# A gated decoder block on one core: the linear recurrence by products of decays, and steps moved between operands and their users

## The chip, the cores and the metric

One Trainium2 chip, one of its cores. The metric is the device time of one execution in microseconds. The core's engines are named as in its profile: PE (TensorE, matmuls; PEld its weight loads), DVE (VectorE), ACT (ScalarE), POOL (GpSimd) and SP (SyncE, which here only issues the loads of weights).

## What is computed

One layer of a decoder block for 256 positions of width 2048, in float32. The part that the change rewrites is the second branch, a gated linear recurrence with 8 heads and 128 keys and values each. Cut to what matters:

```python
a = rmsnorm(h, norm_mix_pre)
q_a, k_a, v_a, q_r, f_r, i_r, g_r, gate_a, gate_r = split(a @ w_in)
# attention: three head groups with windows and dilations, rotary q and k
q = silu(q_r); f = lb + (1 - lb) * sigmoid(f_r)
# S_t = diag(f_t) S_{t-1} + (1 - f_t) v_t^T ;  o_t = S_t^T q_t
r = rmsnorm_per_head(o) * gain * silu(g_r)
y = sigmoid(gate_a) * (attn @ w_pa) + sigmoid(gate_r) * (r @ w_pr)
h = h + rmsnorm(y @ w_o)
h = h + rmsnorm(swiglu(rmsnorm(h)))
```

Without the state, o_t is a sum over all s up to t of (q_t · D(t, s) · k_s) v_s, where D(t, s) is, for each of the 128 keys, the product of the decays f between s and t. Both kernels compute the 256 x 256 matrix of these scores block by block and multiply it with v.

## The kernel before

**Weights.** Nearly all the time goes into products of activations with weights that come from memory once. Each float32 factor is split into a high part (rounded to PE's fp32r format) and the rest, and three of the four partial products are computed. SP loads weights `N_RAW` = 3 units ahead. `split` makes the high part on ACT (L297, `w<-raw`) and the low part on DVE (L298, `w<-raw,w`), two steps ahead of their use (`AHEAD`), into three buffers (`N_SPLIT`). So ACT's split of step n+2 can begin when PE has finished step n-1.

**Blocks and steps.** A block is one slice of a weight matrix. Kind "N" has activations as the stationary operand and 512 columns of weights moving. Kind "W" (the forget gate f, the recurrence's q, and q and k of the attention) has 128 x 128 weights as the stationary operand and positions moving, so that the result stands with channels on the partitions. For each weight tile of a "W" block there is a pair of matmuls (L319 to L321): the high part times both halves of x (512 columns), then the low part times the high half of x (256 columns). One step of "W" is 4 x 2 pairs. "Wide" blocks use a seven-product scheme for 2 x 2 tiles.

**The order of the work** is the order in which the main loop (L1390 to L1421) writes it: for each step first the split of step n+2, then the matmuls of step n, then one advance of each queue of smaller work. `evacs` holds the evacuations of finished blocks, `turns` the transposes of y, and two lanes hold the longer jobs: the opening (norm of x, gates' bounds), the two halves of the recurrence (lane 0) and the eight attention heads (both lanes, as they come free). These jobs are generators: a `yield` ends what is written after one step. Every engine runs its own instructions strictly in the order written.

**The recurrence** (L840 to L1017, one call for four heads): `kk` = 1 - f; f is bounded below (L853), its logarithm taken (L855), and summed within blocks of 64 by a scan on DVE (L857) into `b`. For each block size w = 1, 2, ... 32 (`level`, L861) POOL subtracts the value at the block's middle (L865), ACT takes exponentials (L868, L869), DVE multiplies the left half by kk (L871) and POOL the right half by q (L872); 8 matmuls follow, and DVE copies the scores under a mask into `at` (L883). `level64` and `level128` do the same for the larger distances; `same` (L946) gives the diagonal: q times kk on POOL (L949), summed over the keys by a matmul with a column of ones, and copied under the identity as a mask (L955). A new level begins every second advance, so that two or three are under way. Then come the products with v, the norm (L143 to L151), the gate and the transposes into `recT`.

**Other places that the change touches.** `evac_f` (L717, L718) and `evac_qr` (L734, L735) multiply on DVE and take a sigmoid on ACT at once. `evac_g` (L750 to L756) makes the gate g and stores it to memory from ACT's queue (L756); its multiply L755 needs the row `gainr` from memory. `evac_rope` (L776, L783, L784) writes q and k of the attention (`qk`) and, after the last of a pair of heads, starts `attention`, whose first instructions are matmuls on `qk`. `evac_attn_branch` (L1038, L1039) makes y and hands it to the transposes (L482) in the same step.

Of the kernel before, what the change touches and what calls it, by code (L numbers as in the profile page):

```python
# [30 lines left out]
F_MIN = 2.0 ** -63  # L31
# [60 lines left out]
def tile_hybrid_block(ctx: ExitStack, tc: tile.TileContext, t, out):  # L92
# [100 lines left out]
    def fslot(s):  # L193
        return pool["now"].tile([P, 1024], F32, tag="f", bufs=15, name=nm(s))
# [8 lines left out]
    reset = kp.tile([P, 1024], F32, name="reset")  # L203
    nc.gpsimd.memset(reset, 1.0)
    nc.gpsimd.memset(reset.rearrange("p (n w) -> p n w", w=64)[:, :, 0:1], 0.0)
# [94 lines left out]
    def multiply(st):  # L300
# [257 lines left out]
    def flush_lanes():  # L558
        while work or lanes[0] or lanes[1]:
            advance_lanes()  # L560

# [147 lines left out]
    def evac_f(half):  # L709
        def ev(i, src):  # L710
# [6 lines left out]
            nc.vector.tensor_mul(in_time(d), by_side(src), by_side(by_rows(rowb, 2)))  # L717
            nc.scalar.activation(d, d, AF.Sigmoid)  # L718
# [9 lines left out]
    def evac_qr(half, then=None):  # L728
        def ev(i, src):
# [4 lines left out]
            nc.vector.tensor_mul(in_time(d), by_side(src), by_side(by_rows(rowb, 2)))  # L734
            nc.scalar.activation(s, d, AF.Sigmoid)  # L735
# [6 lines left out]
    def evac_g(half):  # L742
        def go(banks):
# [3 lines left out]
            for i in range(2):  # L747
# [8 lines left out]
                nc.scalar.dma_start(there[:, i, :], dst[:, i, :])  # L756
# [35 lines left out]
    def attention(pair, hh):  # L792
        o, head = None, 2 * pair + hh
        while (head // 4, 2) not in vN:
# [45 lines left out]
    def recurrence(half):  # L840
        q, f, g = qT[half], fT[half], gN[half]
# [3 lines left out]
        def spans(x, w):  # L845
            return x.rearrange("p (n w) -> p n w", w=w)

        kk, b, at = fslot("kk"), fslot("b"), fslot("at")
# [4 lines left out]
        nc.vector.tensor_scalar(f, f, F_MIN, None, op0=OP.max)  # L853
        yield
        nc.scalar.activation(f, f, AF.Ln)  # L855
        yield
        nc.vector.tensor_tensor_scan(  # L857
            out=b, data0=reset, data1=f, initial=0.0, op0=OP.mult, op1=OP.add,
        )
        yield  # L860
        def level(lev, w):  # L861
            x = fslot("x")
            xv, bv, kv, qv = (spans(a, 2 * w) for a in (x, b, kk, q))
            n = 1024 // (2 * w)
            nc.gpsimd.tensor_sub(xv, bv, bv[:, :, w - 1 : w].to_broadcast([P, n, 2 * w]))  # L865
            yield
            left, right = slice(0, w), slice(w, 2 * w)
            nc.scalar.activation(xv[:, :, left], xv[:, :, left], AF.Exp, scale=-1.0)  # L868
            nc.scalar.activation(xv[:, :, right], xv[:, :, right], AF.Exp)  # L869
            yield  # L870
            nc.vector.tensor_mul(xv[:, :, left], xv[:, :, left], kv[:, :, left])  # L871
            nc.gpsimd.tensor_mul(xv[:, :, right], xv[:, :, right], qv[:, :, right])  # L872
            yield
            yield
            ps = aux()
            for e in range(8):
                xe = x[:, e * P : (e + 1) * P]
                mm(
                    spans(ps[:, e * 64 : (e + 1) * 64], w), xe,
                    spans(xe, 2 * w)[:, :, right], True, True,  # L880
                )
            yield
            nc.vector.copy_predicated(  # L883
                at.rearrange("p (e n w) -> p e n w", e=8, w=2 * w)[:, :, :, right],
                lmask[:, lev, :].rearrange("p (n w) -> p n w", w=w)[:, None, :, :]
                .to_broadcast([P, 8, 64 // w, w]).bitcast(I32),
                ps.rearrange("p (e n w) -> p e n w", e=8, w=w),
            )

        def level64():  # L890

            x = fslot("x")
            xe, be, ke, qe = (
                a.rearrange("p (e c t) -> p e c t", e=8, c=2) for a in (x, b, kk, q)
            )
            nc.gpsimd.tensor_sub(
                xe[:, :, 0, :], be[:, :, 0, :], be[:, :, 0, 63:64].to_broadcast([P, 8, 64])
            )
            yield
            nc.scalar.activation(xe[:, :, 0, :], xe[:, :, 0, :], AF.Exp, scale=-1.0)  # L900
            nc.scalar.activation(xe[:, :, 1, :], be[:, :, 1, :], AF.Exp)
            yield
            nc.vector.tensor_mul(xe[:, :, 0, :], xe[:, :, 0, :], ke[:, :, 0, :])
            nc.gpsimd.tensor_mul(xe[:, :, 1, :], xe[:, :, 1, :], qe[:, :, 1, :])
            yield
            ps = aux()
            for e in range(8):
                mm(ps[:64, e * 64 : (e + 1) * 64], xe[:, e, 0, :], xe[:, e, 1, :], True, True)
            yield
            nc.scalar.activation(  # L910
                at.rearrange("p (e t) -> p e t", e=8)[:64, :, 64:],
                ps[:64].rearrange("p (e t) -> p e t", e=8), AF.Copy,
            )

        def level128():

            x = fslot("x")
            xc, bc = (a.rearrange("p (h c t) -> p h c t", h=4, c=4) for a in (x, b))
            end = small("end")
            nc.vector.tensor_add(end[:, :4], bc[:, :, 0, 63], bc[:, :, 1, 63])  # L920
            nc.vector.tensor_sub(
                xc[:, :, 0, :], bc[:, :, 0, :], end[:, :4, None].to_broadcast([P, 4, 64])
            )
            nc.gpsimd.tensor_sub(
                xc[:, :, 1, :], bc[:, :, 1, :], bc[:, :, 1, 63:64].to_broadcast([P, 4, 64])
            )
            nc.gpsimd.tensor_add(
                xc[:, :, 3, :], bc[:, :, 3, :], bc[:, :, 2, 63:64].to_broadcast([P, 4, 64])
            )
            yield  # L930
            xh, kh, qh = (a.rearrange("p (h t) -> p h t", h=4) for a in (x, kk, q))
            nc.scalar.activation(xh[:, :, :P], xh[:, :, :P], AF.Exp, scale=-1.0)
            nc.scalar.activation(xc[:, :, 2, :], bc[:, :, 2, :], AF.Exp)
            nc.scalar.activation(xc[:, :, 3, :], xc[:, :, 3, :], AF.Exp)
            yield
            nc.vector.tensor_mul(xh[:, :, :P], xh[:, :, :P], kh[:, :, :P])
            nc.gpsimd.tensor_mul(xh[:, :, P:], xh[:, :, P:], qh[:, :, P:])
            yield
            ps = aux()
            for h in range(4):  # L940
# [544 lines left out]
```

## Time and profile before

| | us |
|---|---|
| three runs | 1752.32, 1753.49, 1754.23 |
| the profiled execution | 1753.41 |
| its span in the profile | 1751.3 |

Rows of the trace name the source line, the engine, the operation and the tiles (`out<-in`). A busy PE includes matmuls whose ends are modelled. "Idle before" is the time an engine stood still before an instruction, with the line whose end released it.

### The profile page before, as it was taken

The numbers are of one execution on the slowest core, as the hardware profiler recorded it, in microseconds if no ns is written. First come the engines' busy times: TensorE is split into PE (matmuls) and PEld (weight loads), VectorE is DVE, ScalarE is ACT, GpSimd is POOL, SyncE is SP. The second block draws the span as 40 slices with busy tenths as digits, with TensorE's granted clock in tenths as the row PEclk, the third lists the DMA queues.
The fourth block names the chain that finished last, engine by engine and source line by source line (L and its number), as shares of the span: only waits on it lengthen the run. The fifth ranks groups of instructions, "written<-read, shape, count | busy, mean of one in ns | idle before, by whom it ended". The sixth has DMA issues, their size and how long they took to land.

```text
span 1751.3 us, 21627 instructions
## 1 busy us (share of the span) xinstructions
PE 1716.4 (98%) x8357; PEld 1438.6 (82%) x8357; DVE 1382.7 (79%) x1457; ACT 925.6 (53%) x1051; POOL 92.5 (5%) x72
## 2 busy tenths in 40 slices
PE   9999999999989899999999999999999999999997
PEld 7788888888878798888887877888888888888886
DVE  6668888885777897776656467888888888898998
ACT  6445555554645444444444456555555555565663
POOL 0000000000241341000000000000000000000000
PEclk9999999999999999999999999999999999999999
DMA  7766666666535445565545745555555555666553
GB/s 262 248 232 210 224 216 232 235 229 228 166 123 168 158 135 192 166 216 174 181 153 166 264 168 193 192 194 203 204 198 206 197 192 192 216 217 215 189 197 120
DMA packets 208998, 344.78 MB, mean 197 GB/s; under 512 B 10960, under 2 KB 77696, under 8 KB 208896
## 3 DMA queue, kind: packets, MB, share of 16 engines
q1 hardware_dynamic: 198848, 319.41, 54.0%
q10 hardware_dynamic: 7456, 14.56, 2.2%
q0 software_dynamic: 2592, 9.44, 1.6%
q8 instruction: 65, 1.06, 0.2%
q14 instruction: 37, 0.30, 0.1%
HBM read 331.83 MB, written 11.53 MB: 196 GB/s over the span
## 4 chain that ended last, share of the span: by engine, by line
PE 90%; DVE 4%; ACT 2%; issue 1%; POOL 1%; DMA 0%; ACTq 0%; SPq 0%; DVEq 0%; POOLq 0%
PE acc L133 57%; PE aux L133 32%; DVE w L298 1%; ACT w L297 1%; PE aux L821 0%; PE aux L494 0%; DVE x L871 0%; POOL x L865 0%; PE acc L1178 0%; DVE fz L1305 0%; DVE b L857 0%; DMA x<-in_x 0%; PE aux L1178 0%; PE aux L482 0%; DVE sum L783 0%
## 5 line engine op out<-in xcount | busy, mean ns | idle before, releaser
L298 DVE TENSOR_TENSOR w<-raw,w 128x1024 fp32r<-128x1024 f32 (+1 forms) x225 | 279.3, 1243 | 194.2 <-ACT w L297 193.7
L133 PE MATMUL acc<-xT,w 128*128 128x512 f32 (+1 forms) x2048 | 376.4, 343 | 2.9 <-DVE w L298 2.4
L297 ACT ACTIVATE w<-raw 128x1024 fp32r<-128x1024 f32 (+1 forms) x225 | 236.1, 1053 | 254.0 <-PE acc L133 228.0
L133 PEld LDWEIGHTS acc<-xT,w 128*128 128x128 f32 x2048 | 316.2, 190 | 48.8 <-DVE w L298 3.0
L333 DVE TENSOR_TENSOR wl<-raw,w 128x2048 fp32r<-128x2048 f32 x125 | 285.7, 2287 | 62.1 <-ACT w L331 61.1
L331 ACT ACTIVATE w<-raw 128x2048 fp32r<-128x2048 f32 x125 | 238.7, 1910 | 129.8 <-PE aux L133 60.0
L349 DVE TENSOR_TENSOR wl<-sum,w 128x2048 fp32r<-128x2048 f32 x63 | 144.4, 2291 | 65.0 <-ACT w L345 64.9
L133 PE MATMUL acc<-w,hT 128*128 128x512 f32 x622 | 182.5, 392 | 1.5 <-DVE w L298 1.2
L133 PE MATMUL acc<-w,xT 128*128 128x512 f32 x536 | 158.2, 398 | 2.3 <-ACT w L297 1.8
L342 ACT ACTIVATE w<-sum 128x1024 fp32r<-128x1024 f32 x63 | 67.0, 1063 | 172.1 <-DVE sum L337 161.8
L133 PEld LDWEIGHTS acc<-w,hT 128*128 128x128 f32 x622 | 115.8, 188 | 26.9 <-DVE w L298 2.5
L133 PE MATMUL aux<-w,hT 128*128 128x512 f32 x430 | 135.7, 389 | 0.0
L133 PEld LDWEIGHTS acc<-w,xT 128*128 128x128 f32 x536 | 101.9, 192 | 24.5 <-ACT w L297 2.0
L133 PE MATMUL aux<-w,xT 128*128 128x512 f32 x386 | 121.1, 390 | 0.0
L351 DVE TENSOR_TENSOR dl<-raw,dh 128x1536 fp32r<-128x1536 f32 x63 | 110.3, 1751 | 0.0
L133 PEld LDWEIGHTS aux<-w,hT 128*128 128x128 f32 x430 | 80.7, 188 | 16.7
L348 ACT ACTIVATE dh<-raw 128x1536 fp32r<-128x1536 f32 x63 | 92.8, 1474 | 0.0
L133 PE MATMUL acc<-w,yT 128*128 128x512 f32 x384 | 88.1, 390 | 0.2 <-DVE w L298 0.2
L133 PEld LDWEIGHTS aux<-w,xT 128*128 128x128 f32 x386 | 72.4, 188 | 15.3 <-ACT w L331 0.3
L133 PEld LDWEIGHTS acc<-w,yT 128*128 128x128 f32 x384 | 71.9, 188 | 15.5 <-DVE w L298 0.6
L133 PE MATMUL aux<-wl,hT 128*128 128x512 f32 x215 | 83.7, 389 | 0.0
L133 PE MATMUL acc<-w,a 128*128 128x512 f32 x268 | 83.7, 389 | 0.0
(281 smaller groups left out, 2778.2 us busy)
## 6 DMA issues: line engine op xcount, KB each, us to landing
raw<-in_w_in SPq DMA_DIRECT2D x271, 512.0 KB, 4.6
raw<-in_w_ffn_gate_up SPq DMA_DIRECT2D x176, 512.0 KB, 4.4
raw<-in_w_ffn_down SPq DMA_DIRECT2D x88, 512.0 KB, 4.8
raw<-in_w_mix_out SPq DMA_DIRECT2D x32, 512.0 KB, 4.9
kept<-e ACTq DMA_DIRECT2D x32, 256.0 KB, 4.5
raw<-in_w_hgrn_branch SPq DMA_DIRECT2D x16, 512.0 KB, 4.4
raw<-in_w_attn_branch SPq DMA_DIRECT2D x16, 512.0 KB, 4.5
v<-kept POOLq DMA_DIRECT2D x8, 512.0 KB, 6.3
```

The lines of the kernel that those rows point to most:

```text
L133: nc.tensor.matmul(ps, lhsT, rhs, start=start, stop=stop, skip_group_check=True)
L297: nc.scalar.activation(wh[:, k], raw[:, k], AF.Copy)
L298: nc.vector.tensor_sub(wl[:, k], raw[:, k], wh[:, k].bitcast(F32))
L331: nc.scalar.activation(hi, raw, AF.Copy)
L333: nc.vector.tensor_sub(lo, raw, hi.bitcast(F32))
L342: nc.scalar.activation(hi[:, :1024], s[:, :1024], AF.Copy)
L348: nc.scalar.activation(dhi, d, AF.Copy)
L349: nc.vector.tensor_sub(lo, s, hi.bitcast(F32))
L351: nc.vector.tensor_sub(dlo, d, dhi.bitcast(F32))
```

## The change

Recurrence: no logarithms, no scan, no sums. `q` and `kk` are kept, in place, multiplied by the decays up to the edge of their block: q first by its own f, then, from block size to block size, the right half's q by the total decay of the left half, and the left half's kk by that of the right half. The totals (`tot`) are products of pairs of totals. So the scores of a level are plain matmuls of `kk` and `q` as they stand at that level. All multiplies are DVE's; POOL keeps one memset per half, and ACT two copies of scores. Levels run one after the other, three advances each. The diagonal comes from full 128-column products of kk and q, of which the identity mask picks the diagonal.

Besides: for every second weight tile of a "W" block the short matmul goes ahead of the long one; a `yield` stands ahead of the sigmoids in `evac_f` and `evac_qr` and at the start of `attention`; the transposes of y are handed over one advance later; g is stored from POOL's queue; the pool of 4 KB tiles has 16 buffers in place of 15 and the constant `reset` is gone; ahead of the second wide block only lane 1 is flushed.

```diff
-                mm(b.banks[s], h, both, first, False)
-                mm(b.banks[s][:, :S], l, xh, False, last)
+                pair = [(b.banks[s], h, both), (b.banks[s][:, :S], l, xh)]
+                for i, (ps, x, y) in enumerate(pair if k % 2 == 0 else pair[::-1]):
+                    mm(ps, x, y, first and i == 0, last and i == 1)
...
# evac_f, evac_qr
             nc.vector.tensor_mul(in_time(d), by_side(src), by_side(by_rows(rowb, 2)))
+            yield
             nc.scalar.activation(d, d, AF.Sigmoid)
...
# evac_g
-                nc.scalar.dma_start(there[:, i, :], dst[:, i, :])
+                nc.gpsimd.dma_start(there[:, i, :], dst[:, i, :])
...
# attention
         o, head = None, 2 * pair + hh
+        yield
...
# recurrence
+        kk, tot, at = fslot("kk"), fslot("tot"), fslot("at")
         nc.gpsimd.memset(at, 0.0)
-        nc.scalar.preload_act_table_set("natural_log_exp_and_others")
         nc.vector.tensor_scalar(kk, f, -1.0, 1.0, op0=OP.mult, op1=OP.add)
         yield
+        yield
+        own = [aux(), aux()]
+        for e in range(8):
+            es = slice(e * P, (e + 1) * P)
+            mm(own[e // 4][:, e % 4 * P : (e % 4 + 1) * P], kk[:, es], q[:, es], True, True)
+        yield
...
+        nc.vector.tensor_mul(q, q, f)
+        yield
+        yield
...
+        a2, t, at0 = [], f, 0
+        for lev in range(8):
+            w = 1 << lev
+            yield from products(lev, w)
+            if w == P:
+                break
...
+            nc.vector.tensor_mul(qv[:, :, w:], qv[:, :, w:], left)
+            yield
+            nc.vector.tensor_mul(kv[:, :, :w], kv[:, :, :w], right)
+            if w < 64:
+                tv = t.rearrange("p (n two) -> p n two", two=2)
+                t, at0 = tot[:, at0 : at0 + n], at0 + n
+                nc.vector.tensor_mul(t, tv[:, :, 0], tv[:, :, 1])
+            yield
+        yield
...
# evac_attn_branch
-                if i == 1:
-                    turns.append(yT[0].turned(y, 2 * j, 2))
                 yield
+            turns.append(yT[0].turned(y, 2 * j, 2))
...
-                  pre=flush_lanes if n == 1 else None)
+                  pre=(lambda: flush(lanes[1])) if n == 1 else None)
```

In `products`, matmuls of `kk` with the right halves of `q` are followed, one advance later, by the masked copy as before.

How the order moves, at three places. First ACT, where the evacuation of q for heads 4 and 5 falls among the levels of the first half. `sum` and `sig` belong to that evacuation, `x` to the levels, `w<-raw` is the split of weights. Before:

```order
L239 ACTIVATE sum_3699<-acc_3557 128x256
L239 ACTIVATE sum_3699<-acc_3558 128x256
L735 ACT_TABLE_LOAD
L735 ACTIVATE sig_3705<-q_3704 128x512
L868 ACT_TABLE_LOAD
L868 ACTIVATE x_3674<-x_3674 128x64x8
L869 ACTIVATE x_3674<-x_3674 128x64x8
L297 ACTIVATE w_3711<-raw_3508 128x1024
L297 ACTIVATE w_3745<-raw_3555 128x1024
```

And now, at the same place:

```order
L235 ACTIVATE sum_3688<-acc_3555 128x256
L235 ACTIVATE sum_3688<-acc_3556 128x256
L293 ACTIVATE w_3698<-raw_3509 128x1024
L730 ACTIVATE sig_3694<-q_3693 128x512
L293 ACTIVATE w_3721<-raw_3553 128x1024
L293 ACTIVATE w_3752<-raw_3553 128x1024
```

The exponentials and the two table loads are gone, and the split of weights stands ahead of the sigmoid instead of behind it.

Second DVE at the same place, where L298 (now L294) is the low part of the split and L883 (now L884) the masked copy. Before:

```order
L883 COPY_PREDICATED at_3402<-lmask,aux_3663 128x256x2
L298 TENSOR_TENSOR w_3711<-raw_3508,w_3711 128x1024
L737 TENSOR_TENSOR q_3704<-q_3704,sig_3705 128x512
L871 TENSOR_TENSOR x_3674<-x_3674,kk_3400 128x64x8
L298 TENSOR_TENSOR w_3745<-raw_3555,w_3745 128x1024
L883 COPY_PREDICATED at_3402<-lmask,aux_3732 128x128x4
```

And now:

```order
L884 COPY_PREDICATED at_3420<-lmask,aux_3656 128x256x2
L919 TENSOR_TENSOR q_3279<-q_3279,tot_3419 128x256x2
L294 TENSOR_TENSOR w_3698<-raw_3509,w_3698 128x1024
L921 TENSOR_TENSOR kk_3418<-kk_3418,tot_3419 128x256x2
L925 TENSOR_TENSOR tot_3419<-tot_3419 128x256
L294 TENSOR_TENSOR w_3721<-raw_3553,w_3721 128x1024
L732 TENSOR_TENSOR q_3693<-q_3693,sig_3694 128x512
L294 TENSOR_TENSOR w_3752<-raw_3553,w_3752 128x1024
L884 COPY_PREDICATED at_3420<-lmask,aux_3743 128x128x4
```

A level has two multiplies and a product of totals on DVE where it had one multiply, and takes three splits where it took two.

Third PE in the second block of the attention's branch, where y of the block before is transposed (L482, now L479). Before:

```order
L133 MATMUL acc_7162<-w_7124,attnT_2967 128x512 x6
L133 MATMUL acc_7163<-w_7124,attnT_2967 128x512 x6
L133 MATMUL acc_7162<-w_7141,attnT_2968 128x512 x6
L133 MATMUL acc_7163<-w_7141,attnT_2968 128x512 x6
L482 MATMUL aux_7205<-ident,y_7184 128x128 x4
L133 MATMUL acc_7162<-w_7157,attnT_2969 128x512 x6
```

And now:

```order
L132 MATMUL acc_7087<-w_7045,attnT_2964 128x512 x6
L132 MATMUL acc_7088<-w_7045,attnT_2964 128x512 x6
L132 MATMUL acc_7087<-w_7066,attnT_2965 128x512 x6
L132 MATMUL acc_7088<-w_7066,attnT_2965 128x512 x6
L132 MATMUL acc_7087<-w_7082,attnT_2966 128x512 x6
L132 MATMUL acc_7088<-w_7082,attnT_2966 128x512 x6
L479 MATMUL aux_7147<-ident,y_7109 128x128 x4
```

The first four transposes stand behind three steps of the block instead of two.

More of the change, by code (lines that the diff above doesn't have):

```diff
@@ L193, in fslot @@
     def fslot(s):
[L194 removed]
+        return pool["now"].tile([P, 1024], F32, tag="f", bufs=16, name=nm(s))
     def ptile(s):
@@ L890, in level64 @@
[L890 to L940, printed above, removed]
-                mm(ps[:, h * P : (h + 1) * P], xh[:, h, :P], xh[:, h, P:], True, True)
-            yield
-            a2.append(ptile("a2"))
-            nc.scalar.activation(a2[0], ps, AF.Copy)
@@ L946, in same @@
-        def same():
-            x = fslot("x")
-            nc.gpsimd.tensor_mul(x, q, kk)
-            yield
-            ps = aux()
-            for e in range(8):
-                mm(ps[:, e : e + 1], x[:, e * P : (e + 1) * P], ones[:, 0:1], True, True)
-            yield
-            nc.vector.copy_predicated(
-                at.rearrange("p (e t) -> p e t", e=8),
-                ident[:, None, :].to_broadcast([P, 8, P]).bitcast(I32),
-                ps[:, :8, None].to_broadcast([P, 8, P]),
-            )
@@ L961, in recurrence @@
-        a2 = []
-        todo = [level(lev, w) for lev, w in enumerate(LEVELS)] + [same(), level64(), level128()]
-        running, turn = [], 0
-        while todo or running:
-            if turn % 2 == 0 and todo:
-                running.append(todo.pop(0))
-            for r in list(running):
-                try:
-                    next(r)
-                except StopIteration:
-                    running.remove(r)
-            turn += 1
-            yield
+        for i, ps in enumerate(own):
+            nc.vector.copy_predicated(
+                at[:, i * 512 : (i + 1) * 512].rearrange("p (e t) -> p e t", e=4),
+                ident[:, None, :].to_broadcast([P, 4, P]).bitcast(I32),
+                ps.rearrange("p (e t) -> p e t", e=4),
+            )
@@ new lines, in recurrence, with products @@
+        yield
+        nc.vector.tensor_mul(q, q, f)
+        yield
+        yield
+        def products(lev, w):
+            ps = aux()
+            if w < 64:
+                for e in range(8):
+                    es = slice(e * P, (e + 1) * P)
+                    mm(
+                        spans(ps[:, e * 64 : (e + 1) * 64], w), kk[:, es],
+                        spans(q[:, es], 2 * w)[:, :, w:], True, True,
+                    )
+                yield
+                nc.vector.copy_predicated(
+                    at.rearrange("p (e n w) -> p e n w", e=8, w=2 * w)[:, :, :, w:],
+                    lmask[:, lev, :].rearrange("p (n w) -> p n w", w=w)[:, None, :, :]
+                    .to_broadcast([P, 8, 64 // w, w]).bitcast(I32),
+                    ps.rearrange("p (e n w) -> p e n w", e=8, w=w),
+                )
+            elif w == 64:
+                for e in range(8):
+                    k0, q0 = e * P, e * P + 64
+                    mm(ps[:64, e * 64 : (e + 1) * 64], kk[:, k0:q0], q[:, q0 : q0 + 64], True, True)
+                yield
+                nc.scalar.activation(
+                    at.rearrange("p (e t) -> p e t", e=8)[:64, :, 64:],
+                    ps[:64].rearrange("p (e t) -> p e t", e=8), AF.Copy,
+                )
+            else:
+                for h in range(4):
+                    k0, q0 = h * S, h * S + P
+                    mm(ps[:, h * P : (h + 1) * P], kk[:, k0:q0], q[:, q0 : q0 + P], True, True)
+                yield
+                a2.append(ptile("a2"))
+                nc.scalar.activation(a2[0], ps, AF.Copy)
```

46 lines of the change are left out of this document (7 added, 39 removed).

## The prediction

> **What bounds the kernel now.** I read first the page's share of each engine, then the list of who waited for whom on TensorE, then a table of seven stretches of the span.
>
> ```profile
> PE 1716.4 (98%) x8357; PEld 1438.6 (82%) x8357; DVE 1382.7 (79%) x1457; ACT 925.6 (53%) x1051; POOL 92.5 (5%) x72
> ```
>
> TensorE (PE) is busy nearly all the time, so a gain can only come out of its idle time, of a slower clock, or of matmuls that follow each other more slowly than they need. VectorE (DVE) is next with 79%, GpSimd (POOL) hardly works at all. The waits of PE (total us, times, longest) say where the idle time is:
>
> ```profile
> PE aux L133 <- DVE qk L784: 7.4, 3, 6.7
> PE acc L133 <- DVE w L298: 4.2, 6, 1.3
> PE aux L133 <- POOL x L949: 3.7, 1, 3.7
> PE aux L482 <- DVE y L1039: 3.6, 4, 0.9
> PE acc L133 <- ACT w L297: 2.3, 2, 1.8
> ```
>
> Every one of these five is a step that the change touches or a weight split that stands behind such a step. The stretches: from:to, their length, busy us of PE, PE's weight loads, DVE, ACT, POOL, then the granted clock, the DMA share and GB/s.
>
> ```profile
> 64.00:440.00 376.00, 376.00 (x1714) 313.01 (x1713) 293.81 (x238) 200.19 (x173) 3.15 (x4) 1.00 0.66 229
> 44.00:64.00 20.00, 15.76 (x53) 11.41 (x52) 13.47 (x27) 9.63 (x11) 0.85 (x1) 0.83 0.57 200
> 472.00:520.00 48.00, 41.12 (x240) 35.59 (x240) 37.27 (x32) 25.47 (x33) 24.57 (x11) 0.93 0.35 111
> 580.00:612.00 32.00, 25.30 (x138) 22.06 (x138) 26.48 (x26) 14.16 (x21) 12.29 (x6) 0.89 0.41 133
> 612.00:700.00 88.00, 88.00 (x577) 79.30 (x576) 73.82 (x97) 40.09 (x75) 27.36 (x18) 1.00 0.49 161
> 700.00:855.00 155.00, 154.32 (x916) 135.88 (x915) 112.97 (x163) 69.80 (x104) 4.33 (x6) 1.00 0.57 187
> 905.00:955.00 50.00, 46.36 (x217) 37.47 (x216) 33.16 (x39) 21.72 (x24) 0.00 (x0) 1.00 0.52 169
> ```
>
> The first row is an undisturbed stretch, and the one at 612 is another: no idle time, full clock. The others lose 4.2, 6.9, 6.7, 0.7 and 3.6 us to waiting; in three the clock is also down, which costs busy time x (1 - clock): 15.76 x 0.17 = 2.7, 41.12 x 0.07 = 2.9, 25.30 x 0.11 = 2.8 us. The stretches at 472 and 580 are the two recurrences, and there POOL is at work; so I compared DVE's instructions between 470 and 720 with those between 735 and 850, where POOL is nearly idle (busy us, mean ns):
>
> ```profile
> L298 DVE TENSOR_TENSOR w<-raw,w 128x1024 fp32r<-128x1024 f32 x67 | 86.7, 1293 | 46.5 <-ACT w L297 46.2
> L776 DVE TENSOR_TENSOR w<-sum,tabs 64x512 f32<-64x512 f32 x28 | 23.5, 838 | 0.8
> L784 DVE TENSOR_TENSOR qk<-sum,w 128x512 f32<-128x512 f32 x13 | 14.6, 1122 | 0.5
> ...
> L871 DVE TENSOR_TENSOR x<-x,kk 128x512 f32<-128x512 f32 x11 | 11.9, 1083 | 0.1
> L883 DVE COPY_PREDICATED at<-lmask,aux 128x512 f32<-128x512 int32 x12 | 11.0, 918 | 0.1
> L737 DVE TENSOR_TENSOR q<-q,sig 128x512 f32<-128x512 f32 x2 | 5.3, 2644 | 0.0
> ...
> L857 DVE TENSOR_TENSOR_SCAN b<-reset,f 128x1024 f32<-128x1024 f32 x1 | 2.3, 2283 | 0.0
> ```
>
> ```profile
> L298 DVE TENSOR_TENSOR w<-raw,w 128x1024 fp32r<-128x1024 f32 x36 | 44.1, 1225 | 33.4 <-ACT w L297 33.4
> L776 DVE TENSOR_TENSOR w<-sum,tabs 64x512 f32<-64x512 f32 x18 | 12.3, 686 | 0.5
> L241 DVE TENSOR_TENSOR sum<-acc,sum 128x256 f32<-128x256 f32 x18 | 6.7, 416 | 0.0
> L784 DVE TENSOR_TENSOR qk<-sum,w 128x512 f32<-128x512 f32 x9 | 6.2, 692 | 0.4
> ```
>
> The same 512-element multiply-add is 692 ns away from POOL and 1122 ns on average beside it, and L737 even 2644 ns. ACT, in turn, waits inside its own queue (stretch 470 to 620) and reloads tables:
>
> ```profile
> ACT x L868 <- POOL x L865: 9.7, 4, 2.6
> ...
> ACT sig L735 <- DVE q L734: 9.0, 2, 4.6
> ```
>
> While ACT stands there, the high half of the next weights (L297) stands behind it, and then DVE's low half (L298), and then PE. That is how the recurrence, off the path itself, reaches PE.
>
> **The change part by part, against the profiled execution's 1753.4 us** (span 1751.3, 2.1 outside it; the median of the runs is 1753.5, the same).
>
> *Recurrence.* Gone: all of POOL's subtractions and products, the scan, Ln and exponentials, 8 of 19 table loads. Added on DVE: a half has 14 multiplies of 512 elements (at L784's 692 ns in the quiet stretch, 9.7 us), one of 1024 (L298's 1225), six shorter ones (together at most 2 us) and two diagonal copies in place of one; gone are the scan (2.3), eight multiplies of 512 (5.5) and two short passes. So DVE's clean work grows by at most 9.7 + 1.2 + 2.0 - 2.3 - 5.5 = 5.1 us a half, and loses the collisions: eleven L871 at 1083 instead of 692 save 4.3 us, thirteen L784 5.6, twenty-eight L776 4.3, two L737 3.9, together some 18 us over both halves. Does DVE keep up? A step of a wide block costs it 1.23 for the split and a quarter of 2 x 0.42 + 4 x 0.69, 2.1 us; a level takes three steps and adds 0.92 + 2 x 0.69 + 0.42 = 2.7: 9.1 us. PE's three steps need three times eight pairs at 0.349 us (below) and the level's 16 passes at 22.9 / 192 = 0.12 us, 10.3 us:
>
> ```profile
> L133 PE MATMUL aux<-x 128*128 128x64 f32 x192 | 22.9, 272 | 0.3 <-DVE x L871 0.2
> ...
> L133 PE MATMUL aux<-ones,x 128*128 128x1 f32 x32 | 5.4, 299 | 3.7 <-POOL x L949 3.7
> ...
> L133 PE MATMUL aux<-x 128*128 128x128 f32 x16 | 2.1, 274 | 0.0
> ```
>
> DVE is then at 88% of PE's time, near, but below. The diagonal's 16 matmuls grow from 1 column to 128, yet 32 passes at 2.1 / 16 = 0.13 us are 4.2 us against 5.4 before: nothing. I take the whole loss of the stretch at 472: 6.9 + 2.9 = **9.8 us**. Sigmoids put a step behind their operand leave ACT's queue free (the 9.0 us above); behind them stands only the next split, a step early.
>
> *Attention starts a step later.* The 6.7 us wait is for L784. The chain of waits has two collisions just ahead of it (start, us):
>
> ```profile
> 595.30 2.28 DVE w L776
> ...
> 601.37 2.27 DVE qk L784
> ```
>
> They are 1.6 us longer than the 0.69 of the quiet stretch each, and the scan (2.3) goes; what is left, 6.7 - 2.3 - 3.2 = 1.2 us, lies under the 2.8 us of the step that now stands between. So the stretch at 580 gives 6.7 + 2.8 = **9.5 us**, the later heads' waits **0.7**. The last two heads end a step later too, one step ahead of their user; if that cover failed it would cost the 1.2 us of a split.
>
> *Transposes of y a step later.* Between their operand and them now lie 12 matmuls:
>
> ```profile
> 912.61 2.76 PE acc L133 x12
> ```
>
> 2.76 us against waits of 0.9: **3.6 us** go.
>
> *The stores of g move from ACT's queue to POOL's.* The chain of waits in the early stretch (start, us):
>
> ```profile
> 46.52 0.70 DVE g L755
> ...
> 47.25 0.36 ACTq L756
> ...
> 49.01 0.04 DVE w L298
> ```
>
> ACT held the next split behind the store, which waits for L755. Without that, L298 follows L755 at 47.2 instead of 49.0: **1.8 us**. On POOL nothing stands behind the stores before the recurrence's memset. I do not count the rest of that stretch (2.4 us of waiting, 2.7 of clock), since DVE stays as late as it was for what follows.
>
> *Order of the pairs.* In a wide block a 512- and a 256-column matmul alternate; now two long and two short ones follow each other. The price per pair comes from two unbroken runs of the recurrence's stretch, and that of equal long ones from the first projection behind the mix:
>
> ```profile
> 547.79 19.42 PE acc L133 x112
> ...
> 570.91 11.31 PE acc L133 x64
> ```
>
> ```profile
> 976.97 57.20 PE acc L133 x251
> ```
>
> 30.73 us for 88 pairs are 349 ns a pair; 57.20 / 251 = 228 ns for a long matmul, so 342 for a pair with no loss. There are 1024 pairs: at most 7.2 us to gain. No row shows two short ones in a row, and a loss as large is the other bound; a weight load may be what is late behind a short matmul, and then one of two long ones is freed of it, so I take half and a little, **4 us**. [...]
>
> *One answer, nothing:* a 16th buffer, `reset` dropped, `flush(lanes[1])` in place of all lanes (the first lane is empty there), one further yield in the evacuations.
>
> Sum: 9.8 + 9.5 + 0.7 + 3.6 + 1.8 + 4 = 29.4. The busy time has modelled ends, so these idle times are somewhat low; I set that against small new waits: 1753.4 - 29.4 = **1724 us**.
>
> **The rivals.**
> *Pairs give nothing:* all else as above, 1728. For it: the loss is only 7 ns a pair. Chance 0.22.
> *New waits in the recurrence:* multiplies stand in place, so each level's matmuls wait for two of DVE's steps, with less than one step's slack where rope (1.4 us) falls on the same step. If 14 levels wait 1 us each, 1738. Chance 0.18. Against: between 612 and 700 most of the second half's levels run beside rope, with 27 us of POOL in DVE's way, and PE is busy for 88.00 of 88 us.
> *DVE becomes the bound (slower):* decided where a level's 9.1 us exceed PE's 10.3, so when DVE's work is 13% dearer than its rows. Then each of 14 levels waits for a split and a rope step, 1.2 + 1.4 = 2.6 us: 36 us; and at the 0.89 clock of the stretch at 580, 14 levels of 10.3 us lose 0.11 of 144, 16 us: 1753.4 - 29.4 + 52 = 1776. Against: POOL, which made those rows dear, is gone. Chance 0.06.
> *The early clock returns as well:* if the shorter wait keeps the clock up, 2.7 us more: 1721. Against: a faster PE only reaches the next late split sooner, as DVE is behind there. Chance 0.05. [...]
> *No change:* the waits are really for weights in transit. Against: no wait of PE names a DMA, and the DMA share in the bad stretches (0.35, 0.41) is the lowest. 1753, chance 0.04.
>
> **How the numbers follow.** The forecast has 0.45 (its own range 1716 to 1731). Below it I allow the full 7.2 us of the pairs, the early stretch, and idle time that is counted low: 1713. Above it, new waits of 14 us and pairs that give nothing, nearly 1742; 1741 leaves out about the slower rival, no change and a little, under 2 in 10. A measurement of this kernel can tell about 0.2%, 3.5 us: faster 0.90, same 0.04, slower 0.06.
>
> **What would show it.** In the changed kernel's profile: clock 1.00 and no idle time where the recurrences lie; L784's successor at 0.69 us throughout; no wait of PE for qk, y or POOL; the stretch near 47 us shorter by 1.8; an unbroken run of pairs at 345 ns. Wrong if PE waits for q or kk at the levels, if DVE's multiplies are over 0.7 us without POOL, or if the gain comes mainly from the pairs.

## The result and the profile after

| | us |
|---|---|
| the changed kernel, median of 6 runs | 1723.86 (1722.29 to 1724.89) |
| the kernel before beside it, 6 runs | 1753.86 (1752.32 to 1755.21) |
| ratio | 0.9827, 95% interval 0.9815 to 0.984 |
| profiled execution of the changed kernel, and its span | 1723.16, 1721.4 |

The change takes 30.0 us off; the forecast was 1724.0, with 29.4 us off. What the prediction calls a "wide block" where it speaks of pairs of matmuls is a "W" block. The source lines of the changed kernel stand a few lines higher: L133 is now L132, L297 and L298 are L293 and L294, L784 is L779, L755 and L756 are L750 and L751, L482 is L479.

First the engines' shares (page, part 1), to be held against the row that the prediction quotes first.

```profile
PE 1705.4 (99%) x8357; PEld 1431.0 (83%) x8357; DVE 1356.9 (79%) x1477; ACT 895.9 (52%) x1007; POOL 21.7 (1%) x38
```

POOL has gone from 92.5 to 21.7 us. DVE has 20 instructions more and yet 26 us less to do: its clean work grew, its collisions went (what they came to is told further down). All of TensorE's waits (us in total, times, longest):

```profile
PE acc L132 <- DVE w L294: 3.0, 5, 0.8
PE aux L132 <- DVE warm L156: 1.2, 1, 1.2
PE acc L132 <- ACT w L293: 1.1, 1, 1.1
PE aux L491 <- DVE h L1064: 0.8, 1, 0.8
PE aux L132 <- DVE wl L330: 0.4, 1, 0.4
PE acc L132 <- ACT hT L498: 0.3, 1, 0.3
```

The waits for `qk`, for POOL's `x` and for `y` are gone, and no wait for `q` or `kk` at the levels came in their place. The stretches (from:to, length, busy us of PE, PEld, DVE, ACT, POOL, clock, DMA share, GB/s):

```profile
44.00:64.00 20.00, 16.77 (x62) 11.83 (x61) 15.21 (x28) 10.15 (x11) 1.26 (x2) 0.91 0.58 190
...
472.00:520.00 48.00, 48.00 (x306) 42.97 (x305) 35.02 (x49) 18.82 (x25) 0.00 (x0) 1.00 0.48 153
580.00:612.00 32.00, 32.00 (x208) 28.82 (x207) 27.18 (x36) 11.04 (x17) 0.73 (x1) 1.00 0.60 192
879.00:929.00 50.00, 50.00 (x238) 41.36 (x237) 35.80 (x41) 23.26 (x26) 0.00 (x0) 1.00 0.56 178
```

Where PE was busy for 41.12 of 48 and 25.30 of 32 us at clocks of 0.93 and 0.89, it is busy throughout at 1.00, and does 306 matmuls instead of 240 and 208 instead of 138. The stretches are the same in time, not in work: the changed kernel is some 26 us ahead where y is made, so its row for that begins at 879 instead of 905 (its transposes of y run from 888 to 927 us). There PE is busy for 50.00 of 50 us instead of 46.36. Of these four only the stretch at 44 still has idle time and a low clock. DVE's groups between 460 and 700 us:

```profile
L294 DVE TENSOR_TENSOR w<-raw,w 128x1024 fp32r<-128x1024 f32 x70 | 85.7, 1224 | 53.1 <-ACT w L293 52.7
L771 DVE TENSOR_TENSOR w<-sum,tabs 64x512 f32<-64x512 f32 x28 | 19.2, 686 | 0.9
...
L779 DVE TENSOR_TENSOR qk<-sum,w 128x512 f32<-128x512 f32 x14 | 9.7, 692 | 0.5
...
L919 DVE TENSOR_TENSOR q<-q,tot 128x512 f32<-128x512 f32 x12 | 8.3, 691 | 0.0
L921 DVE TENSOR_TENSOR kk<-kk,tot 128x512 f32<-128x512 f32 x12 | 8.2, 687 | 0.1
```

These multiplies of 512 elements take 0.69 us on average here, the new ones as well; 1122 ns on average was L779's predecessor.

From the starts of the first matmul of each part in the two traces one can see where the 29.9 us of the spans went:

| part | before, us | after, us | difference |
|---|---|---|---|
| start to the first "W" block | 397.3 | 396.3 | -1.1 |
| all "W" blocks (recurrences, attention's start) | 444.1 | 420.0 | -24.0 |
| products with `recT` | 51.4 | 50.8 | -0.6 |
| attention's branch, output product | 144.5 | 140.1 | -4.4 |
| the rest | 714.1 | 714.3 | +0.2 |

### The profile page after: what moved, and what is told of

The parts are those of the page before. It is cut to its first block, busy times and chain, and to the rows that moved or that the text cites. A ratio compares the mean times of both kernels' runs of the same rounds, so it can differ in the third digit from the quotient of the medians.

```text
span 1721.4 us, 21535 instructions
## 1 busy us (share of the span) xinstructions
PE 1705.4 (99%) x8357; PEld 1431.0 (83%) x8357; DVE 1356.9 (79%) x1477; ACT 895.9 (52%) x1007; POOL 21.7 (1%) x38
## 4 chain that ended last, share of the span: by engine, by line
PE 96%; DVE 1%; ACT 1%; DMA 1%; issue 0%; SPq 0%; DVEq 0%; ACTq 0%
PE acc L132 62%; PE aux L132 33%; PE aux L491 0%; DVE w L294 0%; PE aux L817 0%; DMA gpost<-in_norm_mix_post 0%; PE acc L1131 0%; DVE fz L1258 0%; ACT w L293 0%; PE aux L1131 0%; PE aux L479 0%; ACT junk L1212 0%; DVE e L1208 0%; ACT junk L1105 0%; DVE wl L330 0%
## 5 line engine op out<-in xcount | busy, mean ns | idle before, releaser
L294 DVE TENSOR_TENSOR w<-raw,w 128x1024 fp32r<-128x1024 f32 (+1 forms) x225 | 274.1, 1219 | 188.0 <-ACT w L293 187.2
L293 ACT ACTIVATE w<-raw 128x1024 fp32r<-128x1024 f32 (+1 forms) x225 | 237.1, 1055 | 289.1 <-PE acc L132 250.2
L132 PE MATMUL acc<-xT,w 128*128 128x256 f32 (+1 forms) x2048 | 370.4, 339 | 0.0
L132 PEld LDWEIGHTS acc<-xT,w 128*128 128x128 f32 x2048 | 311.6, 188 | 43.3
L132 PE MATMUL acc<-w,hT 128*128 128x512 f32 x622 | 182.5, 392 | 1.5 <-DVE w L294 1.2
L132 PE MATMUL acc<-w,xT 128*128 128x512 f32 x536 | 157.3, 395 | 2.7 <-DVE w L294 1.5
L132 PEld LDWEIGHTS acc<-w,hT 128*128 128x128 f32 x622 | 115.8, 188 | 27.0 <-DVE w L294 2.5
L132 PE MATMUL aux<-w,hT 128*128 128x512 f32 x430 | 135.6, 389 | 0.0
L132 PEld LDWEIGHTS acc<-w,xT 128*128 128x128 f32 x536 | 100.6, 189 | 24.9 <-DVE w L294 2.6
L132 PE MATMUL aux<-w,xT 128*128 128x512 f32 x386 | 121.1, 389 | 0.0
L132 PEld LDWEIGHTS aux<-w,hT 128*128 128x128 f32 x430 | 80.7, 188 | 16.7
L132 PE MATMUL acc<-w,yT 128*128 128x512 f32 x384 | 88.2, 390 | 0.3 <-DVE w L294 0.3
L132 PEld LDWEIGHTS aux<-w,xT 128*128 128x128 f32 x386 | 72.6, 188 | 15.1
L132 PEld LDWEIGHTS acc<-w,yT 128*128 128x128 f32 x384 | 71.8, 188 | 15.5 <-DVE w L294 0.7
L132 PE MATMUL aux<-w,a 128*128 128x512 f32 x268 | 83.7, 389 | 0.0
L132 PE MATMUL acc<-w,a 128*128 128x512 f32 x268 | 83.7, 389 | 0.0
```

Of the source, the lines that this page charges most:

```text
L132: nc.tensor.matmul(ps, lhsT, rhs, start=start, stop=stop, skip_group_check=True)
L293: nc.scalar.activation(wh[:, k], raw[:, k], AF.Copy)
L294: nc.vector.tensor_sub(wl[:, k], raw[:, k], wh[:, k].bitcast(F32))
```

## The experiments

Theory: the recurrence's collisions of DVE with POOL made operands late; late operands held ACT's queue and the splits; that held PE. The rival explanations differ in which part of the change cured it: fewer collisions (the new recurrence), more distance between operand and user (the moved steps), ACT's lighter load, or the order of the pairs. Each kernel was timed against the kernel before on its own chip; ratios compare across them.

| kernel | median us | ratio, 95% interval |
|---|---|---|
| changed, old order of pairs | 1725.33 | 0.9838 (0.9824, 0.9851) |
| before, new order of pairs | 1752.81 | 0.9988 (0.9979, 0.9997) |
| before, new recurrence | 1732.19 | 0.9876 (0.9863, 0.989) |
| before, all moved steps | 1731.35 | 0.9871 (0.9857, 0.9884) |
| before, sigmoids moved | 1740.97 | 0.9924 (0.9911, 0.9936) |
| before, attention's start moved | 1751.46 | 0.9981 (0.9972, 0.999) |
| changed, attention's start back | 1725.02 | 0.9836 (0.9822, 0.9849) |
| changed, work on POOL | 1733.40 | 0.9882 (0.9867, 0.9897) |
| changed, work on ACT | 1723.16 | 0.982 (0.9805, 0.9835) |
| changed, work on both | 1733.52 | 0.9878 (0.9862, 0.9895) |
| changed, POOL only writes | 1722.99 | 0.9818 (0.9804, 0.9831) |
| changed, gain row loaded early | 1721.40 | 0.9811 (0.9796, 0.9826) |

### The new recurrence alone

The kernel before with the new `recurrence` and the 16th buffer; sigmoids, attention, y, g and pairs as before.

> The kernel before with the new recurrence alone (16 buffers, no reset constant); pairs, sigmoids, attention's start, y and the store of g as before. My theory: the recurrence's work on GpSimd and ScalarE is what made the operands late, so its stretch gives 9.8 us and the attention's wait shrinks from 6.7 to little over 1 us a pair of heads: about 1736. Rival (the steps put between are what helps, the rewrite is cheaper but hidden): 1748 or more.

Measured: 21.5 us off (1732 instead of the 1736 expected). Its waits of PE:

```profile
PE aux L479 <- DVE y L994: 3.6, 4, 0.9
PE aux L133 <- DVE wl L330: 1.8, 1, 1.8
PE acc L133 <- DVE w L295: 1.7, 3, 0.8
...
PE aux L133 <- DVE qk L781: 0.4, 1, 0.4
```

The wait for `qk` fell from 7.4 to 0.4 us with attention where it was. The "W" blocks take 422.1 us, as in the changed kernel with the old order of pairs (422.4): beside the new recurrence the moved steps add nothing there.

### All moved steps alone

The kernel before with its old recurrence and pairs, and these edits:

```diff
# evac_f, evac_qr, ahead of the sigmoid; attention, ahead of its first matmuls
+            yield
...
# evac_attn_branch
-                if i == 1:
-                    turns.append(yT[0].turned(y, 2 * j, 2))
                 yield
+            turns.append(yT[0].turned(y, 2 * j, 2))
...
# evac_g
-                nc.scalar.dma_start(there[:, i, :], dst[:, i, :])
+                nc.gpsimd.dma_start(there[:, i, :], dst[:, i, :])
```

> The kernel before with the moved steps alone (yields ahead of the sigmoids and of the attention, y one advance later, g stored from GpSimd's queue), old recurrence and old pairs. My theory: y 3.6, the store 1.1 to 1.8, and 2.8 of the attention's 6.7 us with some of the clock, about 5; the recurrence's own 9.8 us stay: 1743. Rival (the steps are what helps): all but the pairs' 5 us comes, 1729.

Measured: 22.3 us off; my 1743 was wrong and the rival near. The collisions are all still there (DVE's groups between 460 and 700 us):

```profile
L778 DVE TENSOR_TENSOR w<-sum,tabs 64x512 f32<-64x512 f32 x26 | 24.3, 934 | 0.8
L874 DVE TENSOR_TENSOR x<-x,kk 128x512 f32<-128x512 f32 x12 | 14.7, 1226 | 0.1
...
L739 DVE TENSOR_TENSOR q<-q,sig 128x512 f32<-128x512 f32 x2 | 5.3, 2672 | 0.0
```

But PE no longer waits for what they delay; of the waits for `qk` and POOL's `x` this is left:

```profile
PE aux L133 <- DVE qk L786: 2.5, 1, 2.5
```

So 21.5 and 22.3 us alone, 30 us together: half of the gain could be had either way. A wait is lateness less slack. The new recurrence takes the lateness away, the moved steps give slack, and each ends the same waits. In the "W" blocks the steps alone save 16.1 us (428.0 instead of 444.1), the recurrence alone 22.0, both without the new pairs 21.7.

### The sigmoids' step alone, attention's step alone

Two kernels, each the one before with only the `yield` ahead of the sigmoids, or only that of `attention`. The first moves the sigmoid and all that stands behind it in the same evacuation by a step.

> The kernel before with one edit: a step between the multiply and the sigmoid in the evacuations of f and of the recurrence's q, so that the weight split stands ahead of the sigmoid in ACT's queue. Theory A (ACT standing in its queue for the late multiply is what passed the collisions on to PE): the first recurrence's stretch gets 9 to 12 us shorter, as in the kernel with all the moved steps: 1742 to 1745. Theory B (ACT's waits for POOL's subtractions, 9.7 us in the same stretch, and the table loads remain and are enough): under 5 us, 1749 or more.

> The kernel before with one edit: attention starts one advance after its operand's last multiply. In the kernel before, PE waits 6.7 us for qk at that place and the clock there costs 2.8 us. Theory A (one late operand, one step in front of it: the recurrence with its collisions stays as it was, and moving the consumer by a 2.8 us step leaves 2.5 us of waiting, as in the kernel with all the moved steps): 4 to 8 us gained, 1746 to 1750. Theory B (the wait is handed on, since ACT and DVE are as late as before for the next split): less than 3 us gained, 1751 or more.

Measured: the sigmoids' step 13.8 us, a little over theory A (11.4 of them in the first recurrence, by the starts of matmuls, as forecast there, and 2.0 more at attention's start); attention's 3.3 us, between the two theories (A at least 4, B under 3) and nearer to B in its mechanism. The sigmoids' kernel in the stretch at 472, and the wait that stays:

```profile
472.00:520.00 48.00, 47.91 (x313) 43.08 (x312) 42.61 (x42) 30.13 (x40) 28.17 (x13) 1.00 0.44 142
```

```profile
PE aux L133 <- DVE qk L786: 5.9, 3, 5.3
```

POOL is at work for 28 of these 48 us and still PE has hardly any idle time: what hurt in this stretch was the work that stood close behind a late multiply, not the collisions as such. The split in ACT's queue is one such piece (ACT waited 9.0 us for L734 there; here it waits 3.7, with the split ahead of it). The multiply L737 moves by the same step, and this run does not part the two. Attention's kernel, stretches at 580 and behind it, and the waits of the whole span:

```profile
580.00:612.00 32.00, 29.89 (x179) 26.11 (x178) 30.24 (x27) 13.93 (x19) 15.90 (x7) 1.00 0.42 133
612.00:640.00 28.00, 24.93 (x152) 21.81 (x152) 25.88 (x26) 12.78 (x20) 13.13 (x7) 0.94 0.46 151
```

```profile
PE acc L133 <- DVE w L298: 7.8, 9, 2.1
...
PE aux L133 <- DVE qk L784: 2.1, 1, 2.1
```

`qk` is cured from 7.4 to 2.1, but the waits for splits grow from 4.2 to 7.8, 3.1 of them just behind, where before there were none: by the starts of matmuls 7.2 us are gained up to there and 5.3 given back in the next stretch. DVE, busy for 25.88 of 28 us there, is still behind and is met a step later.

### Attention's step taken back

The changed kernel without the `yield` at the start of `attention`.

> The changed kernel without the yield at the start of the attention. My theory: VectorE is now late by 1.2 us at the first pair of heads, so the matmuls wait 1 to 1.5 us at each of four pairs, without loss of clock: 1727 to 1729. Rival (the yield alone took the 6.7 us and the clock): 1733 or more. Second rival (the rewrite left nothing to cover): 1724.

Measured: 1725.02, within the interval of the changed kernel. One wait appears:

```profile
PE aux L132 <- DVE qk L779: 0.4, 1, 0.4
```

0.4 us is what is left of the 6.7 when the new recurrence is there; I expected 3 to 5.

### Work put back on POOL, on ACT, on both

The changed kernel; per level, POOL subtracts and multiplies on a tile that nobody reads any more (`gainr`), or ACT takes two exponentials on it, or both in a chain as before, in which ACT reads POOL's result. Nothing is left out.

```diff
# recurrence, per level: on POOL
+            nc.gpsimd.tensor_sub(gainr, at, at)
             nc.vector.tensor_mul(qv[:, :, w:], qv[:, :, w:], left)
             yield
...
+                nc.gpsimd.tensor_mul(gainr[:, :512], gainr[:, :512], gainr[:, 512:])
             yield
...
# on ACT instead
+            nc.scalar.activation(gainr[:, :512], at[:, :512], AF.Exp, scale=0.0)
+            nc.scalar.activation(gainr[:, 512:], at[:, 512:], AF.Exp, scale=0.0)
             yield
```

> The changed kernel with work put back on GpSimd alone: per level of six one subtraction of 1024 elements and one product of 512, both with operands in SBUF, on a tile that nobody reads any more; nobody waits for them. Theory A (VectorE held up by GpSimd is what PE waited for): VectorE's 512-element multiplies go from 0.69 to 2 us and more where they meet, PE waits, 8 us or more: 1732 and up. Theory B (ScalarE standing in its own queue is what PE waited for): the multiplies get longer all the same, but PE does not wait, 1724 to 1726.

> The changed kernel with work put back on ScalarE alone: per level of six two exponentials of 512 elements on a dead tile, with the table loads that alternate with the sigmoids (16 in place of 11). Theory A: 1724 to 1725, since ScalarE has room. Theory B: its queue delays the next split by 2.5 us at a level, 4 to 6 us in all: 1728 to 1730.

> The changed kernel with both, in a chain: GpSimd's subtraction, then the two exponentials on its result, then GpSimd's product; no matmul depends on it. Theory A: as with GpSimd alone, 1732 and up. Theory B: ScalarE now waits for GpSimd with the next split behind it, more than the sum of the two alone: 1732 to 1738, with waits of PE for the split of weights.

Measured: POOL's work costs 9.5 us against the changed kernel (1733.40), ACT's nothing (1723.16), both together what POOL's costs alone (1733.52). ACT took two such groups of exponentials (one is shown), and three table loads of 1.28 us stand at the first of them:

```profile
L926 ACT ACTIVATE gainr<-at 128x512 f32<-128x512 f32 x14 | 8.8, 626 | 0.1
...
L926 ACT ACT_TABLE_LOAD x3 | 3.8, 1283 | 0.1
```

With POOL's work, DVE's groups between 460 and 700 us, and the wait that it makes:

```profile
L294 DVE TENSOR_TENSOR w<-raw,w 128x1024 fp32r<-128x1024 f32 x68 | 91.7, 1349 | 40.0 <-ACT w L293 39.4
L771 DVE TENSOR_TENSOR w<-sum,tabs 64x512 f32<-64x512 f32 x26 | 23.4, 898 | 0.8
...
L922 DVE TENSOR_TENSOR kk<-kk,tot 128x512 f32<-128x512 f32 x12 | 10.8, 904 | 0.1
```

```profile
PE aux L132 <- DVE kk L922: 6.7, 5, 3.0
```

The larger groups of multiplies of 512 elements are back at 0.77 (L779) to 0.90 us (L922) on average, splits at 1.35. POOL also reads a tile, `at`, that DVE writes next, but DVE has no wait for POOL between 470 and 720 us in this kernel's list of waits: it is the length of its own instructions that makes it late. Where that reaches PE (stretches, columns as above), in this kernel and then in the changed one:

```profile
470.00:560.00 90.00, 89.30 (x560) 78.98 (x559) 73.28 (x88) 38.73 (x63) 31.29 (x15) 1.00 0.48 158
590.00:690.00 100.00, 93.96 (x583) 83.61 (x582) 84.94 (x105) 35.33 (x51) 32.33 (x19) 0.97 0.45 149
```

```profile
470.00:560.00 90.00, 90.00 (x567) 80.01 (x566) 64.45 (x90) 39.28 (x64) 0.71 (x1) 1.00 0.49 158
590.00:690.00 100.00, 100.00 (x647) 89.59 (x647) 77.51 (x113) 42.52 (x73) 2.14 (x3) 1.00 0.50 163
```

POOL works 31 us in the first and 32 in the second. In the first half's recurrence DVE rises from 72% to 81% of the time and PE loses 0.7 us; in the second's, beside rope and attention, it stands at 78% already, rises to 85%, and PE loses 6.0 us and some clock. DVE's share alone does not tell the two apart: with the sigmoids moved it was busy for 42.61 of 48 us, 89%, and PE lost 0.09. The wait is for `kk`, whose matmuls are written one advance behind its multiply in both stretches; in the second, the work for rope and attention comes between on DVE.

### POOL that only writes

The changed kernel; POOL is kept as busy per level with memsets, and a copy of one column that ties them to the level.

```diff
+            nc.gpsimd.tensor_copy(gainr[:, :1], at[:, :1])
+            nc.gpsimd.memset(gainr, 1.0)
+            nc.gpsimd.memset(gainr, 1.0)
             nc.vector.tensor_mul(qv[:, :, w:], qv[:, :, w:], left)
             yield
...
+            nc.gpsimd.memset(gainr, 1.0)
+            nc.gpsimd.memset(gainr, 1.0)
             yield
```

> The changed kernel with POOL busy per level about as long as in the run with POOL's subtraction and product, but with memsets (about 4 x 0.97 us a level, 54 us in all) and a copy of one column that ties them to the level. Left out: nothing; the tile they write is dead. Theory A (DVE's two-operand multiplies are slowed by POOL's reads of operands): no change, 1723 to 1725, multiplies at 0.69 us. Theory B (any work of POOL slows them): 1730 or more, multiplies at 0.9 us on average as in that run.

Measured: 1722.99, nothing lost. One of the four memsets, and the multiply of DVE beside them:

```profile
L921 POOL MEMSET gainr<- 128x1024 f32 x14 | 13.5, 967 | 0.8
...
L924 DVE TENSOR_TENSOR kk<-kk,tot 128x512 f32<-128x512 f32 x12 | 8.2, 686 | 0.1
```

About 54 us of memsets leave DVE's two-operand multiplies at 0.69 us, where 59 us of subtractions and products put them at 0.77 to 0.90. In the stretch where those cost 6.0 us, POOL is as busy here and PE loses nothing:

```profile
590.00:690.00 100.00, 100.00 (x647) 89.61 (x646) 78.27 (x114) 41.20 (x72) 31.30 (x37) 1.00 0.54 174
```

So for these multiplies it is not POOL's being busy that costs: the subtractions and products do something that memsets do not, they read whole operands and they compute, and the runs do not part the two. DVE's instructions with one large operand are another matter: between 460 and 700 us the four L811 take 646 ns on average in this kernel and 487 in the changed one, the four L716 619 and 408. That cost PE nothing.

### The order of the pairs, both ways round

The changed kernel with the old order, and the kernel before with the new one.

```diff
-                pair = [(b.banks[s], h, both), (b.banks[s][:, :S], l, xh)]
-                for i, (ps, x, y) in enumerate(pair if k % 2 == 0 else pair[::-1]):
-                    mm(ps, x, y, first and i == 0, last and i == 1)
+                mm(b.banks[s], h, both, first, False)
+                mm(b.banks[s][:, :S], l, xh, False, last)
```

> The changed kernel with every pair of matmuls in the old order, long before short. My theory: two equal matmuls in a row save the loss behind a short one; the first 64 pairs of the wide blocks took 22.60 us before and 22.29 after, 4.9 ns a pair, so 1024 pairs give 4.9 us back: 1728.8. Rival (every weight load is hidden in either order, and the 0.3 us come from elsewhere): 1723.9, and 22.29 us for the first 64 pairs as now.

> The kernel before with one edit: the order of the long and short matmuls. The reverse edit on the changed kernel cost 1.5 us, 2.3 us counted over the wide-channel blocks alone. Theory A (5 ns a pair where nothing else holds PE, nothing where it waits for splits anyway): 1 to 3 us gained. Theory B (my forecast's 4 us, or the 4.9 us that 16 times 0.31 us make): 4 to 5 us gained. Theory C (the reverse edit cost something else than the pairs): 0.

Measured: the old order costs 1.5 us where I expected 4.9 (1725.33, intervals overlapping; 2.3 us over the "W" blocks of the two traces), and the new one alone gains 1.9 us (ratio 0.9988, 0.9979 to 0.9997), within theory A. Unbroken runs of pairs in the chain of waits (start, us): first the changed kernel, then the one with the old order.

```profile
398.97 55.97 PE acc L132 x321
...
547.63 19.52 PE acc L132 x112
```

```profile
398.95 57.60 PE acc L132 x326
...
549.75 19.41 PE acc L132 x112
```

The first run of each lies ahead of the recurrence: 55.97 us for 160.5 pairs are 348.7 ns a pair, 57.60 for 163 are 353.4. The second lies beside rope and the levels: 348.6 and 346.6 ns, no gain at all. Averages over the eight pairs of a step, from the starts of matmuls, show the same (old order, then new; ns):

```
ahead of the recurrence     8 pairs 2826 | 2786
from its start on           8 pairs 2845 | 2830
  of that, from the first long matmul of a step to the next   273 | 272
```

Everywhere else in such a step a short matmul follows a long one after 231 to 237 ns on average; this one, the first that needs the step's low half, comes some 38 ns late on average, after 338 ns at most. It is hardly later in the new order, so it explains little of the loss: the new order gains 40 ns a step in the quiet part and 15 in the loaded one, and of these 25 ns the longer wait takes some 4. Most of the rest is that the other pairs of the old order are closer in the loaded part (2807 without the 38 ns, instead of 2826), and why stays open.

### The gain row loaded earlier

The changed kernel; the load of the row that L750 needs is issued ahead of the sums of squares.

```diff
+        nc.sync.dma_start(gainr, t["hgrn_norm_gain"].to_broadcast([P, HW]))
         yield from sumsq(ss, xt)
-        nc.sync.dma_start(gainr, t["hgrn_norm_gain"].to_broadcast([P, HW]))
```

> The changed kernel with the row of gains for g loaded eight steps earlier from the same queue. VectorE stood still for 2.3 us for it at 45 us, and was then behind until the first wide block. My theory: 2.3 us go, and with PE's clock kept up perhaps one more: 1720.5 to 1721.6. Rival (PE is then held by the next late thing, the low half of the first wide split): no more than 1 us, 1723.

Measured: 1721.40, the lowest of all, as expected in size, and below both kernels. It is 2.5 us under the changed kernel's median and 1.8 under the run with ACT's work on the same chip, which lost nothing; the intervals overlap, so this last step is likely, not shown. The chain of waits around the first wide block's split, in the changed kernel and then in this one (start, us):

```profile
58.18 1.92 ACT w L328
60.10 0.02 issue
60.12 2.30 DVE wl L330
```

```profile
55.46 1.93 ACT w L328
57.41 2.31 DVE wl L330
```

The split is 2.7 us earlier; of that, 1.1 us are left at the first "W" block (395.2 instead of 396.3). The last section shows why the two traces compare badly at this place: the opening has two lengths. In the four kernels with the new recurrence and store and the same length of it as here, the "W" blocks begin at 397.0 to 397.6, 1.9 to 2.4 us later than here.

## Why the prediction was right, point by point

**The total** came out 0.6 us from the sum, and the place too: 9.8 + 9.5 + 0.7 + 4 = 24.0 us were forecast for the "W" blocks, 24.0 measured. Inside, two errors cancel: the pairs gave about 2 instead of 4, the waits and the clock about 22 instead of 20. That these come out even is luck. I had set idle time that is counted low against small new waits; the new waits did not come.

**The recurrence, 9.8 us.** Somewhat small: by the starts of matmuls, up to a point in the "W" blocks where both kernels have done the first half of the recurrence and not begun the second, the new recurrence alone gains 12.1 us and the sigmoids' step alone 11.4. The levels bear their multiplies: no wait for `q` or `kk`, DVE at 72% and 78% where I had estimated 88%. DVE's collisions I had put at 18 us from four lines; others collided too (means of the whole span: L298 1248 ns for 1224 now, 223 times; L783 874 for 685, 24 times; L722 801 for 408, 8 times), some 33 us in all. What held PE in this stretch is shown to be the nearness of users to a late multiply, as the prediction said of ACT's queue: the sigmoids' step cures it while the collisions last. With POOL's subtractions and products put back on the changed kernel the second half's recurrence loses instead (6.0 us of waiting). So the collisions are shown as one cause of lateness, and the sigmoids' step shows that distance can keep it from PE.

**Attention starts a step later, 9.5 us.** This is the step that failed. I gave the gain to the moved start; the 6.7 us go whether attention moves or not (0.4 left with its start as before), and on the old recurrence the move alone is worth 3.3 us, because DVE is then met at the next split. At this place the new recurrence is enough by itself, and its freed time on DVE is the likely reason: no run frees DVE alone. I summed terms that share a cause as if each had its own: the 20 us came out since they were counted per stretch, not per edit; per edit my forecast for the moved steps alone was 12 us off.

**Transposes of y, 3.6 us.** Held: no wait for `y` is left, and attention's branch with what follows is 4.4 us shorter, 0.8 more than the waits; the kernel with only the moved steps shows the same (3.4 us up to the output product, 1.0 in it). The 0.6 us less at the products with `recT` were not forecast; attention's step alone, on the kernel before, shows 0.7 there.

**Store of g, 1.8 us.** The chain in the early stretch of the changed kernel (start, us):

```profile
47.32 0.06 DVE g L750
...
47.94 1.21 DVE w L294
```

The gain row arrived 0.8 us later than before (L755 stood at 46.52), and still the split starts at 47.94 instead of 49.01: 1.9 us better against its cause. Over the profiled executions the first "W" block starts at 398.9 us on average with the old store (5 kernels, 397.3 to 400.4) and at 396.8 with the new one (8 kernels, 395.8 to 397.6, the one with the gain row loaded earlier not counted): 2.1 us, no sharper than the spread within each group.

**Order of the pairs, 4 us.** Mis-sized: 1.5 to 2.3, and no run of pairs came down to the 345 ns that I had named as a sign (348.7 and 348.6). In the quiet stretch the order gains (353.4 to 348.7 ns a pair), in the run at 548 us it does not (346.6 and 348.6). That a weight load is what comes late behind a short matmul was a guess of mine; no run shows it. The forecast's 349 ns a pair was the mean of two runs at 346.8 and 353.4 ns, which I took for one price.

**The rivals.** New waits in the recurrence and DVE as the bound: neither occurred; the kernel with POOL's work shows how the first would look, a wait of PE for `kk`. The comparison of DVE's time with PE's, on which the second rests, is no test by itself: DVE was busy for 89% of a stretch in the sigmoids' kernel, and for 73.82 of 88 us in the prediction's own row at 612, without a loss of PE to speak of. The early clock did not come back: the two stretches around the first wide split,

```profile
52.00:60.00 8.00, 6.06 (x22) 4.18 (x21) 5.62 (x17) 4.91 (x7) 0.56 (x1) 0.90 0.53 171
60.00:68.00 8.00, 7.61 (x30) 5.80 (x29) 6.75 (x3) 5.79 (x5) 0.00 (x0) 0.89 0.79 284
```

still run at 0.90 and 0.89. In the 20 us from 44 on PE stood still for 3.2 us (16.77 busy) instead of 4.2, and the clock there is 0.91 instead of 0.83; what sets the clock there no run shows.

## What to carry to other kernels

A wait is lateness less slack, so two edits that work on the same wait do not add (21.5 and 22.3 us alone, 30.0 together): sum by the stretch in which time is lost, and test each edit alone before giving it the credit. An in-order queue that stands behind a late operand passes lateness on to everything written behind it (ACT stood for 9.0 us in front of two sigmoids, with the next splits behind them); one step between the operand and its user was worth 13.8 us with all collisions left in place. Before POOL is given a share of DVE's work, look at what else DVE does in that stretch and how close behind its results their users stand: the same 31 us of POOL cost 0.7 us in one stretch and 6.0 beside rope and attention. DVE's share of the time is no sufficient sign: with the sigmoids moved it was 89%, and PE lost 0.09 us.

## What was not expected of the hardware

The early spell of low clock moves but does not go away. Among the kernels with the new recurrence and the new store, the time from the first wide matmul to the first "W" block is 334.7 us where that matmul starts at 61.1 to 61.6 us, and 337.7 where it starts at 57.4 to 59.9. In the kernel with the gain row loaded early, the clock and PE's wait of this place:

```profile
52.00:60.00 8.00, 4.95 (x19) 3.14 (x18) 5.74 (x12) 6.92 (x8) 0.00 (x0) 1.00 0.48 169
60.00:68.00 8.00, 8.00 (x29) 6.40 (x29) 4.11 (x2) 4.70 (x4) 0.00 (x0) 0.79 0.92 334
```

```profile
PE aux L132 <- DVE wl L330: 1.8, 1, 1.8
```

The low clock now lies behind the first wide split (8.00 x 0.21 = 1.7 us) and the next one is waited for by 1.8 instead of 0.4 us: 3.1 us, which is the difference. In the changed kernel's trace most of the low clock lies ahead of its first wide matmul at 61.6 us (0.71 from 56 to 61.6 us, 0.96 from there to 64). So an earlier opening is worth less than its own chain says. Whether the clock follows from the idle time ahead of it was not tested.
